# Four subtractions per unit move from VectorE to GpSimd in a two-layer encoder trunk

## The chip, the core and the metric

The kernel runs on one core of a Trainium2 chip. The metric is the device time of one execution in microseconds (us); before the change the median of three runs is 2601.45 us (2601.13 to 2602.01). PE is TensorE (matmul), PEld its weight load, DVE VectorE, ACT ScalarE, POOL GpSimd, and SP the queue that issues most of the DMAs.

## What is computed

Two layers over 1024 frames of width 1024 in float32: chunked attention in the first, a gated DeltaNet mixer in the second, and behind each a dense MLP with a residual. The change touches only the MLP, which runs twice:

```python
def squared_relu_mlp(h, w_up, w_down):      # h: 1024x1024, w_up: 1024x4096, w_down: 4096x1024
    return jnp.square(jax.nn.relu(h @ w_up)) @ w_down
```

## The kernel before

Every float32 operand of a product is split into a high part (ACT copies it to the matmul type, `high`) and a low part (the difference, `low`, on DVE or POOL), and a block product is three matmuls per 128 rows: high by high, high by low, low by high. The MLP's two products are blocked two by two with seven products instead of eight (a Strassen-Winograd scheme), so that sums of blocks are needed of weights and of activations.

**Up half** (`up`). It walks through 16 units; a unit takes two panels of `w_up`, 128 columns each. It makes seven block products of 12 matmuls (84 matmuls) in the order Y(11), Z(s1), Y(s2), X(12), Y(s3), Z(s4), Y(22). X's evacuation is the instruction `ssum<-acc` (L1172), and its start is taken as the unit's mark below ("X end"). `put` makes a quarter of the squared activations: add, then ReLU and scale on DVE (L1172, L1174), square on ACT (L1175). The four quarters of a unit are g00, g01, g11, g10. They go to DRAM (`gr`), and `combine` (L1073) makes four differences of them in tiles `c`: t1 = g01 - g00, t3 = g11 - g01, t2 = g11 - t1, t4 = g10 - t2. It splits each into high (ACT) and low (DVE, L1086) and writes both to DRAM (`gt`). `combine` is called at a unit's end for units 0 to 13, and its steps run beside the products of the next unit.

Beside a unit, `up_weights` (L1030) makes the next unit's weights: two loads of 512 KB into the two `wraw` buffers (SP), four sums on POOL (S1, S2, S3, a21: tiles `s` and the first half of the second `wraw`), and the splits: `whi`/`wlo` of 128x1024 for the first panel (w0) and the second (w1), `ahi`/`alo` of 128x512 for s1, s2, s3. There are two `wraw` buffers only, so a panel's load is issued when the `wlo` that reads the old panel last is done. Each engine works its instructions off in the order in which the program issues them; that order is set by where the generators (`sums`, `more`, `rest`) are advanced between the products.

**Down half** (`down`). 32 units of seven products of six matmuls; after each product a *step* advances the generators. `late` is one: after the last residual rows are loaded it runs `late_sums` (L1395), which loads the four quarters of units 14 and 15 back into the halves of `R` and `ssum`, makes the four differences in place, splits them and writes them to `gt`. Seven steps are one unit.

Of the kernel before, what the change touches and what calls it, by code (L numbers as in the profile page):

```python
# [11 lines left out]
ALU = mybir.AluOpType  # L12
# [8 lines left out]
HB = 512  # L21
# [186 lines left out]
class Trunk:  # L208
# [821 lines left out]
    def up_weights(self, i, n, ap, A):  # L1030

        raw = []
        for j in range(2):
            t = self.wp.tile([P, KT, P], F32, name=self.nm("wraw"), tag="wraw")
            self.wq.dma_start(t, self.a["w_up"][i, 2 * n + j])
            raw.append(t)
        a11, a12, a21, a22 = raw[0][:, :4], raw[0][:, 4:], raw[1][:, :4], raw[1][:, 4:]
        yield
        S1, S2, S3 = (ap.tile([P, 4, P], F32, name=self.nm("s"), tag=f"a{m}") for m in range(3))
        A["s1"], A["s2"], A["s3"] = (  # L1040
            [ap.tile([P, 4, P], F32R, name=self.nm("a" + z), tag=f"a{3 + 2 * m + y}")
             for y, z in enumerate(("hi", "lo"))] for m in range(3))
        w0, w1 = ([self.wp.tile([P, KT, P], F32R, name=self.nm("w" + z), tag="w" + z) for z in ("hi", "lo")]
                  for _ in range(2))
        A["11"], A["12"] = ([z[:, 4 * m : 4 * m + 4] for z in w0] for m in range(2))
        A["s4"], A["22"] = ([z[:, 4 * m : 4 * m + 4] for z in w1] for m in range(2))

        self.padd(S1, a21, a22)
        self.psub(S2, S1, a11)
        self.psub(S3, a11, a21)  # L1050
        self.psub(a21, a12, S2)
        yield

        self.high(A["s1"][0], S1)
        self.high(w0[0], raw[0])
        yield

        self.low(A["s1"][1], S1, A["s1"][0])
        self.low(w0[1], raw[0], w0[0])
        self.high(A["s2"][0], S2)  # L1060
        yield

        self.low(A["s2"][1], S2, A["s2"][0])
        self.high(A["s3"][0], S3)
        yield

        self.low(A["s3"][1], S3, A["s3"][0])
        self.high(w1[0], raw[1])
        yield

        self.low(w1[1], raw[1], w1[0])

    def combine(self, n, g, mp, gt, first):  # L1073


        nc = self.nc
        t = {z: mp.tile([P, S], F32, name=self.nm("c"), tag=f"x{4 * (n % 2) + k}") for k, z in enumerate(SUMS)}

        def sub(z, x, y):
            nc.vector.tensor_tensor(t[z][:, HB:], x, y, ALU.subtract)  # L1080

        def high(z):
            self.high(t[z][:, :HB].bitcast(F32R), t[z][:, HB:])

        def low(z):
            nc.vector.tensor_tensor(t[z][:, HB:].bitcast(F32R), t[z][:, HB:], t[z][:, :HB], ALU.subtract)  # L1086
            nc.sync.dma_start(gt[n, SUMS.index(z)], t[z])

        def keep(name, x):
            if n < 2:  # L1090
                h, l = ops[name][n] = self.part(ex, str(n + 2 * (name == "21")))
                self.high(h, x)
                self.low(l, x, h)

        ex, ops = first
        sub("t1", g[0, 1], g[0, 0])
        sub("t3", g[1, 1], g[0, 1])
        yield
        sub("t2", g[1, 1], t["t1"][:, HB:])
        sub("t4", g[1, 0], t["t2"][:, HB:])  # L1100
        high("t1")
        keep("11", g[0, 0])
        yield
        high("t3")
        low("t1")
        keep("21", g[1, 0])
        yield
        high("t2")
        low("t3")
        yield  # L1110
        high("t4")
        low("t2")
        yield
        low("t4")
        yield
# [279 lines left out]
    def late_sums(self, mp, gr, gt):  # L1395

        nc = self.nc
        last = 2 * KT
        u = self.new_R()
        s = self.np.tile([P, S], F32, name=self.nm("ssum"), tag="ssum")  # L1400
        hi = [mp.tile([P, HB], F32, name=self.nm("r"), tag=t) for t in ("r", "q1")]
        for n in (last - 2, last - 1):
            r = u[:, :HB], s[:, :HB], s[:, HB:], u[:, HB:]
            for k, x in enumerate(r):
                nc.sync.dma_start(x, gr[n, k])
            r11, r21, r22, r12 = r
            for _ in range(4):
                yield
            for k, (t, x, y) in enumerate(((r11, r12, r11), (r12, r22, r12), (r22, r22, r11), (r21, r21, r22))):
                nc.vector.tensor_tensor(t, x, y, ALU.subtract)  # L1410
                for _ in range(4):
                    yield
            for z, t in zip(("t1", "t3", "t2", "t4"), (r11, r12, r22, r21)):
                h = hi[0]
                hi.reverse()
                self.high(h.bitcast(F32R), t)
                for _ in range(2):
                    yield
                nc.vector.tensor_tensor(t.bitcast(F32R), t, h, ALU.subtract)
                yield  # L1420
                for k, x in enumerate((h, t)):
                    nc.sync.dma_start(gt[n, SUMS.index(z), :, k * HB : (k + 1) * HB], x)
                for _ in range(3):
                    yield
# [1233 lines left out]
```

## Time and profile before

| | |
|---|---|
| median of three runs | 2601.45 us |
| the profiled execution | 2599.54 us, of which the span of its instructions 2596.4 us |
| PE busy | 2478.9 us (95%) |
| DVE busy | 1962.4 us (76%) |
| ACT busy | 1209.4 us (47%) |
| POOL busy | 1099.2 us (42%) |
| up halves | about 600 to 877 us and 1971 to 2249 us of the span |
| down halves | about 880 to 1175 us and 2252 to 2560 us |

A row of the timeline gives start, duration, engine, line, operation, output and inputs; "x2" marks merged neighbours, and brackets give the idle time of the engine before it and what ended that. A duration is that of the whole instruction with whatever it waits for once it has begun, so the same instruction can show 0.68 us at one place and 1.78 at another. Matmuls are pipelined, and PE's idle time is small everywhere; it is read best from the distance between marks that return once per unit.

### The profile page before, as it was taken

The numbers are of one execution on the slowest core, as the hardware profiler recorded it, in microseconds if no ns is written. First come the engines' busy times: TensorE is split into PE (matmuls) and PEld (weight loads), VectorE is DVE, ScalarE is ACT, GpSimd is POOL, SyncE is SP. The second block draws the span as 40 slices with busy tenths as digits, with TensorE's granted clock in tenths as the row PEclk, the third lists the DMA queues.
The fourth block names the chain that finished last, engine by engine and source line by source line (L and its number), as shares of the span: only waits on it lengthen the run. The fifth ranks groups of instructions, "written<-read, shape, count | busy, mean of one in ns | idle before, by whom it ended". The sixth has DMA issues, their size and how long they took to land.

```text
span 2596.4 us, 36674 instructions
## 1 busy us (share of the span) xinstructions
PE 2478.9 (95%) x12638; PEld 2050.4 (79%) x12638; DVE 1962.4 (76%) x3425; ACT 1209.4 (47%) x2269; POOL 1099.2 (42%) x962
## 2 busy tenths in 40 slices
PE   8999999999999999998888999999899999999997
PEld 6888888787778777886666788888687777777885
DVE  6665656778888788878579976675678888788878
ACT  6666667545545433334663334333335545433333
POOL 2444456412233365566464333332412322356556
PEclk9999999999999999999998999999999999999998
DMA  4222224315555977743443121223324555977752
GB/s 162 67 68 78 61 85 145 134 67 190 195 206 208 348 228 239 235 146 110 119 137 109 53 79 60 64 77 114 114 82 162 199 203 192 346 232 257 232 163 81
DMA packets 193081, 392.42 MB, mean 151 GB/s; under 512 B 54960, under 2 KB 61552, under 8 KB 192896
## 3 DMA queue, kind: packets, MB, share of 16 engines
q1 hardware_dynamic: 176048, 355.46, 41.4%
q10 hardware_dynamic: 16848, 34.63, 3.4%
q8 instruction: 99, 1.62, 0.3%
q14 instruction: 86, 0.70, 0.1%
HBM read 254.06 MB, written 127.57 MB: 147 GB/s over the span
## 4 chain that ended last, share of the span: by engine, by line
PE 55%; DVE 16%; issue 5%; DMA 2%; ACT 2%; POOL 1%; SPq 0%; ACTq 0%; DVEq 0%; POOLq 0%
PE y L1008 21%; PE z L1008 9%; PE acc L163 8%; PE acc L1008 6%; PE tp L163 3%; PE s L163 3%; DVE c L1086 3%; DVE wlo L1014 2%; PE acc L279 2%; PE acc L278 2%; PE acc L277 2%; DVE x L1508 1%; DVE ft L163 1%; DVE ssum L1172 1%; DVE alo L1014 1%
## 5 line engine op out<-in xcount | busy, mean ns | idle before, releaser
L163 PE MATMUL acc<-xs,whi 128*128 128x512 f32 x1808 | 631.1, 412 | 10.3 <-DVE xp L163 9.7
L1023 POOL TENSOR_TENSOR s<-wraw 128x256 f32<-128x256 f32 (+1 forms) x93 | 88.3, 950 | 772.7 <-DMA wraw<-in_w_up_dram 427.5
L163 PEld LDWEIGHTS acc<-xs,whi 128*128 128x128 f32 x1808 | 333.0, 191 | 59.4 <-DVE xp L163 6.5
L163 PE MATMUL acc<-xs,wlo 128*128 128x512 f32 x896 | 368.4, 411 | 2.8 <-POOL wlo L163 2.8
L1008 PE MATMUL y<-xs,whi 128*128 128x512 f32 x1008 | 312.6, 391 | 6.6 <-DVE x L1508 3.2
L163 POOL TENSOR_TENSOR wlo<-wraw,whi 128x512 fp32r<-128x512 f32 x126 | 167.9, 1332 | 244.8 <-ACT whi L163 195.5
L1008 PEld LDWEIGHTS y<-xs,whi 128*128 128x128 f32 x1008 | 188.8, 188 | 48.9 <-DVE x L1508 4.9
L1008 PE MATMUL y<-xs,wlo 128*128 128x512 f32 x504 | 199.7, 396 | 9.2 <-DVE wlo L1014 8.7
L1014 DVE TENSOR_TENSOR wlo<-wraw,whi 128x512 fp32r<-128x512 f32 (+1 forms) x182 | 198.8, 1092 | 8.5 <-ACT whi L1017 8.5
L1017 ACT ACTIVATE whi<-wraw 128x512 fp32r<-128x512 f32 (+2 forms) x191 | 146.5, 767 | 123.9 <-PE y L1008 87.1
L1008 PE MATMUL y<-xs,a 128*128 128x512 f32 x732 | 189.4, 394 | 13.8 <-DVE x L1508 12.6
L1017 ACT ACTIVATE a<-s 128x256 fp32r<-128x256 f32 x122 | 63.9, 524 | 290.4 <-PE y L1008 144.3
L1508 DVE TENSOR_TENSOR x<-y,x 128x512 f32<-128x512 f32 x240 | 165.1, 688 | 39.0 <-PE y L1008 32.4
L163 PEld LDWEIGHTS acc<-xs,wlo 128*128 128x128 f32 x896 | 171.7, 192 | 28.4 <-POOL wlo L163 4.1
L1008 PEld LDWEIGHTS y<-xs,a 128*128 128x128 f32 x732 | 135.1, 188 | 51.8 <-DVE x L1508 22.4
L1008 PE MATMUL acc<-xs,whi 128*128 128x512 f32 x528 | 162.9, 390 | 0.0
L1008 PE MATMUL y<-xs,ahi 128*128 128x512 f32 x512 | 161.9, 397 | 0.9 <-ACT nt L1197 0.9
L1008 PE MATMUL z<-xs,whi 128*128 128x512 f32 x480 | 148.0, 389 | 0.0
L163 POOL TENSOR_SCALAR pr<-pr,rs 128x640 f32<-128x640 f32 (+4 forms) x128 | 88.6, 696 | 129.3 <-DVE rs L163 98.2
L163 DVE CUSTOM_DVE_ANT_0 pr<-sp,bias 128x640 f32<-128x640 f32 (+4 forms) x128 | 83.8, 654 | 63.6 <-PE sp L163 62.6
L1086 DVE TENSOR_TENSOR c<-c 128x512 fp32r<-128x512 f32 x112 | 131.6, 1192 | 0.0
L163 POOL TENSOR_TENSOR cy<-cy,cz 128x512 f32<-128x512 f32 x48 | 69.3, 1443 | 145.3 <-DVE cz L163 135.2
(340 smaller groups left out, 6154.6 us busy)
## 6 DMA issues: line engine op xcount, KB each, us to landing
xs<-gt SPq DMA_DIRECT2D x256, 256.0 KB, 4.6
gt<-c SPq DMA_DIRECT2D x112, 512.0 KB, 4.6
wraw<-in_w_up_dram SPq DMA_DIRECT2D x64, 512.0 KB, 3.9
wraw<-in_w_down_dram SPq DMA_DIRECT2D x64, 512.0 KB, 4.4
r<-gr SPq DMA_DIRECT2D x88, 256.0 KB, 3.4
wraw<-in_w_in_dram SPq DMA_DIRECT2D x32, 512.0 KB, 3.5
gr<-ssum ACTq DMA_DIRECT2D x62, 256.0 KB, 2.0
wraw<-in_w_qkv_dram SPq DMA_DIRECT2D x30, 512.0 KB, 3.4
```

Source lines behind the costliest of these rows:

```text
L163: return call(*args, **more)
L277: nc.tensor.matmul(ps, hi[:, k], xh, start=(k == 0), stop=False)
L278: nc.tensor.matmul(ps, hi[:, k], xl, start=False, stop=False)
L279: nc.tensor.matmul(ps, lo[:, k], xh, start=False, stop=(k == KT - 1))
L1008: nc.tensor.matmul(ps, w[:, k], x, start=bool(first and f), stop=bool(last and e), skip_group_check=True)
L1014: self.nc.vector.tensor_tensor(lo, src, hi.bitcast(F32), ALU.subtract)
L1017: self.nc.scalar.activation(hi, src, AF.Copy)
L1023: self.nc.gpsimd.tensor_tensor(out, x, y, ALU.add)
L1086: nc.vector.tensor_tensor(t[z][:, HB:].bitcast(F32R), t[z][:, HB:], t[z][:, :HB], ALU.subtract)
L1172: nc.vector.tensor_tensor(g, c, t, ALU.add)
L1508: nc.vector.tensor_tensor(x, ps, x, ALU.add)
```

## The change

Three edits. (1) In `combine` the four differences are made on POOL (`psub`, L1020) instead of DVE; their splits stay. (2) In `late_sums` the four differences of units 14 and 15 are made on POOL as well; the first stands 14 steps behind the loads instead of 4, and they stand 3 steps apart instead of 4. (3) In `up_weights` for the third unit on, the last two sums S3 and a21 are issued one step after S1 and S2. All lines from 1050 on move by 1 to 4.

```diff
@@ up_weights
         self.padd(S1, a21, a22)
         self.psub(S2, S1, a11)
-        self.psub(S3, a11, a21)
-        self.psub(a21, a12, S2)
+        if n == 1:
+            self.psub(S3, a11, a21)
+            self.psub(a21, a12, S2)
         yield
...
         self.high(A["s2"][0], S2)
+        if n > 1:
+            self.psub(S3, a11, a21)
+            self.psub(a21, a12, S2)
         yield
@@ combine
         def sub(z, x, y):
-            nc.vector.tensor_tensor(t[z][:, HB:], x, y, ALU.subtract)
+            self.psub(t[z][:, HB:], x, y)
@@ late_sums
-            for _ in range(4):
+            for _ in range(14):
                 yield
             for k, (t, x, y) in enumerate(((r11, r12, r11), (r12, r22, r12), (r22, r22, r11), (r21, r21, r22))):
-                nc.vector.tensor_tensor(t, x, y, ALU.subtract)
-                for _ in range(4):
+                self.psub(t, x, y)
+                for _ in range(3):
                     yield
```

What that makes of the instruction order, first on DVE at the end of a middle unit of the first up half (unit 6, near 708 us; `g` and `ssum` are the quarters, `c` the differences, `wraw_7745` the second panel of the next weights). Before:

```order
L1172 TENSOR_TENSOR g_6885<-z_7710,nt_7764 128x512
L1174 SCALAR_TENSOR_TENSOR g_6885<-g_6885,R_6833 128x512
L1014 TENSOR_TENSOR alo_7787<-s_7782,ahi_7786 128x512
L1174 SCALAR_TENSOR_TENSOR g_6886<-y_7709,R_6833 128x512
L1080 TENSOR_TENSOR c_7860<-g_6885,ssum_6884 128x512
L1080 TENSOR_TENSOR c_7862<-ssum_6884,g_6885 128x512
L1014 TENSOR_TENSOR alo_7789<-s_7783,ahi_7788 128x512
L1080 TENSOR_TENSOR c_7861<-ssum_6884,c_7860 128x512
L1080 TENSOR_TENSOR c_7863<-g_6886,c_7861 128x512
L1014 TENSOR_TENSOR wlo_7793<-wraw_7745,whi_7792 128x1024
L1086 TENSOR_TENSOR c_7860<-c_7860 128x512
L1086 TENSOR_TENSOR c_7862<-c_7862 128x512
```

The same place on DVE now:

```order
L1176 TENSOR_TENSOR g_6885<-z_7710,nt_7764 128x512
L1178 SCALAR_TENSOR_TENSOR g_6885<-g_6885,R_6833 128x512
L1014 TENSOR_TENSOR alo_7787<-s_7782,ahi_7786 128x512
L1178 SCALAR_TENSOR_TENSOR g_6886<-y_7709,R_6833 128x512
L1014 TENSOR_TENSOR alo_7789<-s_7783,ahi_7788 128x512
L1014 TENSOR_TENSOR wlo_7793<-wraw_7745,whi_7792 128x1024
L1090 TENSOR_TENSOR c_7860<-c_7860 128x512
L1090 TENSOR_TENSOR c_7862<-c_7862 128x512
```

The four differences are gone from DVE, and `wlo` of the second panel stands directly behind the last `alo`.

On POOL, from the same unit's weight sums to the next unit's. Before:

```order
L1023 TENSOR_TENSOR s_7781<-wraw_7745 128x512
L1020 TENSOR_TENSOR s_7782<-s_7781,wraw_7743 128x512
L1020 TENSOR_TENSOR s_7783<-wraw_7743,wraw_7745 128x512
L1020 TENSOR_TENSOR wraw_7745<-wraw_7743,s_7782 128x512
L1023 TENSOR_TENSOR s_7939<-wraw_7903 128x512
L1020 TENSOR_TENSOR s_7940<-s_7939,wraw_7901 128x512
L1020 TENSOR_TENSOR s_7941<-wraw_7901,wraw_7903 128x512
L1020 TENSOR_TENSOR wraw_7903<-wraw_7901,s_7940 128x512
```

Now:

```order
L1023 TENSOR_TENSOR s_7781<-wraw_7745 128x512
L1020 TENSOR_TENSOR s_7782<-s_7781,wraw_7743 128x512
L1020 TENSOR_TENSOR s_7783<-wraw_7743,wraw_7745 128x512
L1020 TENSOR_TENSOR wraw_7745<-wraw_7743,s_7782 128x512
L1020 TENSOR_TENSOR c_7860<-g_6885,ssum_6884 128x512
L1020 TENSOR_TENSOR c_7862<-ssum_6884,g_6885 128x512
L1020 TENSOR_TENSOR c_7861<-ssum_6884,c_7860 128x512
L1020 TENSOR_TENSOR c_7863<-g_6886,c_7861 128x512
L1023 TENSOR_TENSOR s_7939<-wraw_7903 128x512
L1020 TENSOR_TENSOR s_7940<-s_7939,wraw_7901 128x512
L1020 TENSOR_TENSOR s_7941<-wraw_7901,wraw_7903 128x512
L1020 TENSOR_TENSOR wraw_7903<-wraw_7901,s_7940 128x512
```

The differences stand between two units' weight sums; the sums themselves keep their order, S3 and a21 directly behind S1 and S2, so edit (3) moves no instruction on POOL.

In the down half of the first block, DVE's rows around the first late difference (in `R`) before (`x` is the residual that a product is added to, `a` a low part of the next weights):

```order
L1508 TENSOR_TENSOR x_9130<-y_9659,x_9130 128x512
L1508 TENSOR_TENSOR x_9130<-acc_9658,x_9130 128x512
L1410 TENSOR_TENSOR R_9668<-R_9668 128x512
L1014 TENSOR_TENSOR a_9715<-s_9686,a_9714 128x256
L1508 TENSOR_TENSOR x_9132<-y_9659,x_9132 128x512
```

POOL's rows from the same difference on now, ten steps later (`xs` are lows of reloaded quarters, `s` and `wraw` weight sums):

```order
L1020 TENSOR_TENSOR R_9668<-R_9668 128x512
L1023 TENSOR_TENSOR s_9861<-wraw_9839 128x256
L1020 TENSOR_TENSOR s_9862<-s_9861,wraw_9839 128x256
L1012 TENSOR_TENSOR xs_9872<-r_9852,xs_9872 128x512
L1020 TENSOR_TENSOR s_9861<-wraw_9839 128x256
L1020 TENSOR_TENSOR wraw_9839<-wraw_9839,s_9862 128x256
L1020 TENSOR_TENSOR R_9668<-ssum_9669,R_9668 128x512
L1012 TENSOR_TENSOR xs_9896<-r_9854,xs_9896 128x512
L1020 TENSOR_TENSOR ssum_9669<-ssum_9669,R_9668 128x512
```

Before, a difference stood on DVE between two additions to the residual; now the four stand on POOL between the lows of reloaded quarters and the weight sums.

## Rows read from the trace of the kernel before

**Rows 1.** The page, busy time of each engine over the span.

```profile
PE 2478.9 (95%) x12638; PEld 2050.4 (79%) x12638; DVE 1962.4 (76%) x3425; ACT 1209.4 (47%) x2269; POOL 1099.2 (42%) x962
```

**Rows 2.** Timeline of PE inside a product: start, us, engine, line, operation.

```profile
702.05 0.61 PE L1008 MATMUL z<-xs,whi 128*128 128x512 f32 x2
...
702.73 0.61 PE L1008 MATMUL z<-xs,whi 128*128 128x512 f32 x2
```

**Rows 3.** Waits of PEld, 560 to 880 us: total us, times, longest.

```profile
PEld y L1008 <- DVE wlo L1014: 10.0, 14, 1.7
PEld y L1008 <- ACT nt L1197: 5.6, 15, 0.8
```

**Rows 4.** Timeline of DVE, the unit mark "X end" in both up halves.

```profile
639.77 0.69 DVE L1172 TENSOR_TENSOR ssum<-acc,nt 128x512 f32<-128x512 f32 x1 [2.97 <-PE acc L1008]
...
738.18 0.69 DVE L1172 TENSOR_TENSOR ssum<-acc,nt 128x512 f32<-128x512 f32 x1 [3.01 <-PE acc L1008]
...
758.05 0.69 DVE L1172 TENSOR_TENSOR ssum<-acc,nt 128x512 f32<-128x512 f32 x1 [2.99 <-PE acc L1008]
...
816.83 0.69 DVE L1172 TENSOR_TENSOR ssum<-acc,nt 128x512 f32<-128x512 f32 x1 [2.97 <-PE acc L1008]
...
836.09 0.69 DVE L1172 TENSOR_TENSOR ssum<-acc,nt 128x512 f32<-128x512 f32 x1 [2.97 <-PE acc L1008]
...
855.64 0.69 DVE L1172 TENSOR_TENSOR ssum<-acc,nt 128x512 f32<-128x512 f32 x1 [2.97 <-PE acc L1008]
...
2011.41 0.69 DVE L1172 TENSOR_TENSOR ssum<-acc,nt 128x512 f32<-128x512 f32 x1 [3.01 <-PE acc L1008]
...
2228.48 0.69 DVE L1172 TENSOR_TENSOR ssum<-acc,nt 128x512 f32<-128x512 f32 x1 [3.00 <-PE acc L1008]
```

**Rows 5.** Timeline of POOL, the first weight sum (S1) of three units.

```profile
718.42 1.29 POOL L1023 TENSOR_TENSOR s<-wraw 128x512 f32<-128x512 f32 x1 [13.33 <-DMA wraw<-in_w_up_dram]
...
738.31 1.29 POOL L1023 TENSOR_TENSOR s<-wraw 128x512 f32<-128x512 f32 x1 [13.48 <-DMA wraw<-in_w_up_dram]
...
816.11 1.29 POOL L1023 TENSOR_TENSOR s<-wraw 128x512 f32<-128x512 f32 x1 [12.60 <-DMA wraw<-in_w_up_dram]
```

**Rows 6.** Timeline of DVE and POOL at 604 us, where they overlap.

```profile
604.33 1.78 DVE L1014 TENSOR_TENSOR alo<-s,ahi 128x512 fp32r<-128x512 f32 x1
...
605.64 1.61 POOL L1020 TENSOR_TENSOR wraw<-wraw,s 128x512 f32<-128x512 f32 x1
...
606.03 2.30 DVE L1014 TENSOR_TENSOR wlo<-wraw,whi 128x1024 fp32r<-128x1024 f32 x1
```

**Rows 7.** Timeline of DVE at the end of unit 6.

```profile
709.22 0.68 DVE L1174 SCALAR_TENSOR_TENSOR g<-y,R 128x512 f32<-128x512 f32 x1
709.82 0.68 DVE L1080 TENSOR_TENSOR c<-g,ssum 128x512 f32<-128x512 f32 x1
...
711.02 0.68 DVE L1014 TENSOR_TENSOR alo<-s,ahi 128x512 fp32r<-128x512 f32 x1
...
713.01 1.22 DVE L1014 TENSOR_TENSOR wlo<-wraw,whi 128x1024 fp32r<-128x1024 f32 x1
```

**Rows 8.** Timeline of ACT and of SP's issues at the same place.

```profile
708.73 0.63 ACT L1175 ACTIVATE g<-g 128x512 f32<-128x512 f32 x1 [3.10 <-DVE g L1174]
...
711.03 1.06 ACT L1017 ACTIVATE whi<-wraw 128x1024 fp32r<-128x1024 f32 x1 [0.46 <-ACT g L1175]
...
707.45 7.14 SPq L1035 DMA_DIRECT2D wraw<-in_w_up_dram  x2
```

**Rows 9.** Windows with late differences: length, then busy PE, PEld, DVE, ACT, POOL.

```profile
930.00:1050.00 120.00, 116.56 (x502) 92.94 (x501) 103.12 (x148) 39.94 (x74) 70.06 (x67) 1.00 0.71 229
...
2300.00:2430.00 130.00, 126.57 (x546) 101.21 (x545) 111.23 (x159) 43.27 (x80) 77.91 (x74) 1.00 0.72 231
```

**Rows 10.** Timeline of DVE and PE around the first late difference.

```profile
932.07 0.87 DVE L1410 TENSOR_TENSOR R<-R 128x512 f32<-128x512 f32 x1
...
935.04 0.73 PE L1008 MATMUL y<-xs,whi 128*128 128x512 f32 x2 [0.89 <-DVE x L1508]
```

## Prediction

> **What bounds the kernel now.** The page first: PE is busy 95% of the span, DVE 76%, POOL 42% [rows 1]. So DVE's sum of work is not the limit; what counts is where PE waits. In an up half I took two distances. Inside a product three matmuls follow each other in 0.68 us (702.05 to 702.73) [rows 2], so the 84 matmuls of a unit need 84 x 0.68 / 3 = 19.04 us. The marks "X end" stand 215.87 us apart over 11 units in the first block (639.77 to 855.64) and 217.07 in the second (2011.41 to 2228.48) [rows 4]: 19.62 and 19.73 us per unit. PE loses 0.58 and 0.69 us per unit, and the waits say to whom: to the low part of the first weight panel on DVE, and to ACT's copies of y and z, which come behind the same DVE work [rows 3].
>
> Why is that low part late? DVE stands idle about 3 us ahead of X end [rows 4], then has a chain to do between X end and `wlo`, and just then POOL makes the weight sums. The rows at 604 us show how the two engines get in each other's way: `alo` takes 1.78 us, POOL's next sum ends 1.14 us after `alo` has ended (606.11 to 607.25), and `wlo` ends 1.08 us after that (608.33) [rows 6]. Alone `alo` takes 0.68, `wlo` 1.22 [rows 7] and a POOL sum 1.29 [rows 5]. So two instructions that read two SBUF tiles on DVE and POOL take turns, each waiting for the other's to end. Hence it matters when POOL's run begins. Two units of the trace show the size: with S1 0.13 us behind X end (738.31 against 738.18) the next mark came after 19.87 us (758.05), with S1 0.72 us ahead of it (816.11 against 816.83) after 19.26 (836.09) [rows 4, 5]. The earlier the weight sums, the more of them falls into DVE's idle 3 us.
>
> **What sets S1.** Its second panel. The load can be issued when the `wlo` of the old second panel is done: that row ends at 713.01 + 1.22 = 714.23 [rows 7], the second of the two issues ends at 707.45 + 7.14 = 714.59 [rows 8], S1 begins at 718.42 [rows 5], 4.19 us behind `wlo`'s end. And `wlo` stands on DVE behind the four differences, while its high part was there at 711.03 + 1.06 = 712.09 [rows 8].
>
> **Part 1: the differences of units 0 to 13 on POOL.** It takes 14 x 4 = 56 subtractions per block, 112 in all, from DVE. That DVE time itself (112 x 0.68 us) is worth nothing, since DVE waits 3 us per unit anyway [rows 4]. Worth something is when `wlo` ends, so I walk through unit 6. g01's square ends at 708.73 + 0.63 = 709.36 [rows 8]; t1 can start at 709.4 and, at 1.3 us, ends at 710.7. `alo` is ready when the row at 709.22 ends, 709.90 [rows 7], waits for t1 and takes about 0.6 more: 711.3. t3 has waited and takes 1.14 [rows 6]: 712.45. `wlo` is ready at 712.09, waits to 712.45 and takes 1.08 [rows 6]: 713.5, against 714.23 now. Then t2 to 714.7, the first `c` low to 715.3, t4 to 716.45, the second `c` low to about 717.0. So the panel is freed 0.7 us earlier, and S1, 4.19 behind it, begins at 717.7; POOL's queue is empty at 716.45, 1.2 us before. DVE is done 1.4 us before the next mark. ACT's highs of the four differences now wait for POOL, but each difference is there before ACT comes to it, with over half a microsecond to spare in this walk.
>
> How sure is the 0.7? `wlo` waits for none or for all of one POOL subtraction, so it ends between 712.09 + 1.08 = 713.2 and 712.09 + 1.14 + 1.08 = 714.3: S1 from 1.0 us earlier to 0.1 later. I take 0.7, from the walk.
>
> With S1 0.7 us ahead of X end the nearest measured unit has 19.26 us. At that pace 11 units take 211.86 us: 4.0 us less in the first block, 5.2 in the second, together 9.2. The bounds: nothing lost on PE at all, 11 x 19.04 = 209.44, is 6.4 + 7.6 = 14.0 us less; no shift is 0. Three more places per block I count as cancelling: units 2 and 14 at the ends of the run gain like the others (0.4 each), unit 1, where the differences of unit 0 stand before the same `wlo` on POOL in a crowded place, may lose up to one POOL subtraction of wait (1.14 us of S1, some 0.8 us of period by the two measured units).
>
> **Part 2: the late differences.** 16 subtractions leave DVE in the down halves, at up to 0.87 us each [rows 10], and 16 come to POOL at 1.3. In the two stretches with late differences PE is idle 120 - 116.56 = 3.44 and 130 - 126.57 = 3.43 us [rows 9], partly because of the splits, which stay. The first difference shows the harm that one can do: behind it the addition to the residual came late and PE stood 0.89 us [rows 10]. On POOL a difference can still hold up a low on DVE by its 1.14 us, so part of that stays. Bounds: all idle time gone, 6.9 us less; or every one of the 16 costs 0.89, 14.2 us instead of 6.9, 7.3 more. I take 2 us less, nearer to no change, as on either engine a difference delays DVE by about the same. The 10 steps of delay themselves cost nothing: the results are read only in the unit before the last quarter of the down half, and 14 steps of six matmuls (1.36 us by [rows 2]) put 19 us between the loads and the first difference.
>
> **Part 3: the weight sums in two runs.** In the order of POOL nothing moves: S3 and a21 stand directly behind S1 and S2 as before. Zero.
>
> **Sum.** 9.2 + 2 = 11.2 us less. The profiled execution of before took 2599.54 us (span 2596.4), so 2588.3 by it; the median of the runs is 1.9 us above that execution, and on its scale it is 2601.45 - 11.2 = 2590.
>
> **A rule against the change.** A subtraction of this size takes 1.29 us on POOL [rows 5] and 0.68 on DVE [rows 7], a ratio of 1.9. The Trainium skill, "GPSIMD Engine Reference", section "Key points", says that for elementwise work the DVE is about twice as fast; the ratio here agrees. By that rule the differences were better left where they are; what would follow from it is the first rival.
>
> **Rivals.** *POOL's run is late (slower).* Place: POOL's queue, where S1 now stands behind t4. If all four differences had to wait for a DVE instruction of `wlo`'s size, they would take 4 x (1.30 + 1.08) = 9.5 us from 709.4 on, to 718.9, and S1 would begin 0.5 us later than now. From 718.42 on it decides. By the two measured units (0.61 us of period per 0.85 us of S1) that is 0.36 us per unit, 22 x 0.36 = 8 us more: 2609. Against it: only one `wlo` stands in that stretch of DVE [rows 7], and the walk ends at 716.45. Chance 0.12.
>
> *No shift (within 0.2%).* `wlo` meets a POOL difference that has just begun and ends at 714.3; the wait for POOL takes the place of the differences in its own queue, and S1 stays. Then only part 2 is left: about 2600. For it: the walk's 712.45 rests on steps of a few tenths. Chance 0.20.
>
> *The down half takes it back (within 0.2%).* Part 2 at its bad end, 7.3 more against 9.2 less: about 2600. Chance 0.06.
>
> **How the numbers follow.** My forecast has 0.62, the rivals 0.12, 0.20 and 0.06. About 0.2%, 5.2 us, is what a measurement here can tell from no change. Faster 0.62, within it 0.26, slower 0.12. The range takes in the best end of both parts (14.0 + 6.9, 2581) and the two rivals near 2600 with the scatter of the runs (2603); left out are the slower rival and a few hundredths.
>
> **What would show it.** Distance of the marks: 19.2 to 19.3 us instead of 19.62 and 19.73. S1 about 0.7 us ahead of X end in nearly every unit. `wlo` of the second panel directly behind POOL's second difference, at about 1.4 us. PEld's waits on DVE `wlo` clearly below 10.0 us. In the down stretches PE idle 2 to 3 us each. The prediction is wrong if `wlo` ends no earlier against X end, if S1 is released by POOL's own queue instead of the load, or if S1 comes earlier and the marks stay where they are.

## The result: 0.9912 of the time before

The changed kernel takes 2579.86 us in the median (2571.49 to 2582.57) against 2601.29 (2600.86 to 2602.01) beside it, a ratio of 0.9912 with a 95% interval of 0.9889 to 0.9935. That is 21.4 us less, where 11.2 were forecast: 2590, with a low end of 2581, so the median lies 1 us below the range. The direction and the place were right; the terms for both halves were too small. The profiled execution took 2579.18 us, its span 2577.4 (before 2599.54 and 2596.4).

The page's line of busy times, against [rows 1], shows about 199 us more on POOL and 48 less on DVE:

```profile
PE 2472.7 (96%) x12638; PEld 2063.6 (80%) x12638; DVE 1914.8 (74%) x3297; ACT 1210.1 (47%) x2269; POOL 1298.2 (50%) x1090
```

The marks "X end" of the changed kernel, the same four as the ends in [rows 4] (timeline: start, duration, engine, line, operation, tiles; in brackets the idle time before):

```profile
641.82 0.69 DVE L1176 TENSOR_TENSOR ssum<-acc,nt 128x512 f32<-128x512 f32 x1 [1.30 <-PE acc L1008]
851.79 0.69 DVE L1176 TENSOR_TENSOR ssum<-acc,nt 128x512 f32<-128x512 f32 x1 [1.79 <-PE acc L1008]
2003.83 0.69 DVE L1176 TENSOR_TENSOR ssum<-acc,nt 128x512 f32<-128x512 f32 x1 [1.29 <-PE acc L1008]
2213.30 0.69 DVE L1176 TENSOR_TENSOR ssum<-acc,nt 128x512 f32<-128x512 f32 x1 [1.53 <-PE acc L1008]
```

The two in each block stand 209.97 and 209.47 us apart, 19.09 and 19.04 per unit. 19.04 is what 84 matmuls need [rows 2]: over most of both up halves PE loses nothing any more. What the parts of the span took in the profiled executions, counted from mark to mark and to the last product of a down half (first block + second block):

| stretch | before | after | difference |
|---|---|---|---|
| up halves, marks of units 1 to 15 | 277.88 + 278.98 | 271.09 + 270.93 | -14.8 |
| down halves, mark 15 to last product | 331.95 + 328.11 | 328.90 + 325.00 | -6.2 |
| the rest of the span, of which the edits move only unit 0's four differences | 1379.5 | 1381.5 | +2.0 |

**The unit that the prediction walked through** (unit 6, the answer to [rows 5, 7, 8]): POOL's differences, DVE from the last `alo` to the next first panel's low, ACT's copy, and SP's two loads and two writes.

```profile
709.29 1.30 POOL L1020 TENSOR_TENSOR c<-g,ssum 128x512 f32<-128x512 f32 x1 [4.96 <-ACT g L1179]
710.55 1.74 POOL L1020 TENSOR_TENSOR c<-ssum,g 128x512 f32<-128x512 f32 x1
712.26 2.27 POOL L1020 TENSOR_TENSOR c<-ssum,c 128x512 f32<-128x512 f32 x1
714.61 1.80 POOL L1020 TENSOR_TENSOR c<-g,c 128x512 f32<-128x512 f32 x1
716.84 1.29 POOL L1023 TENSOR_TENSOR s<-wraw 128x512 f32<-128x512 f32 x1 [0.43 <-DMA wraw<-in_w_up_dram]
...
709.77 1.37 DVE L1014 TENSOR_TENSOR alo<-s,ahi 128x512 fp32r<-128x512 f32 x1
711.97 1.41 DVE L1014 TENSOR_TENSOR wlo<-wraw,whi 128x1024 fp32r<-128x1024 f32 x1 [0.83 <-ACT whi L1017]
714.57 2.39 DVE L1090 TENSOR_TENSOR c<-c 128x512 fp32r<-128x512 f32 x2 [1.19 <-POOL c L1020]
718.24 0.69 DVE L1176 TENSOR_TENSOR ssum<-acc,nt 128x512 f32<-128x512 f32 x1 [1.29 <-PE acc L1008]
724.59 1.21 DVE L1014 TENSOR_TENSOR wlo<-wraw,whi 128x1024 fp32r<-128x1024 f32 x1
...
710.87 1.06 ACT L1017 ACTIVATE whi<-wraw 128x1024 fp32r<-128x1024 f32 x1 [0.46 <-POOL c L1020]
...
707.29 6.44 SPq L1035 DMA_DIRECT2D wraw<-in_w_up_dram  x2
715.28 2.03 SPq L1091 DMA_DIRECT2D gt<-c  x2
```

The second panel's low ends at 713.38 (forecast 713.5), t4 at 716.41 (forecast 716.45): the walk holds to 0.2 us. But S1 begins at 716.84, not 717.7. The load takes 3.46 us from that low to S1, not 4.19. And the first write of a difference is issued at 715.28, 1.55 us behind the load's issue (713.73); before, it was issued at 714.85, 0.26 us behind it. With S1 1.40 us ahead of X end, the next first panel's low ends at 725.80, 7.56 us behind X end; before it was 8.67.

What waits in the first up half (waiter <- what it waited for: us, times, longest), against [rows 3]:

```profile
DVE wlo L1014 <- ACT whi L1017: 11.3, 13, 1.4
...
PEld y L1008 <- DVE wlo L1014: 4.6, 5, 1.8
...
PEld y L1008 <- ACT nt L1201: 2.5, 6, 0.6
```

PE's wait for `wlo` is less than half of 10.0. It is now DVE that waits, for ACT's copy of the second panel.

### The profile page after: what moved, and what is told of

It reads as the page before. It is cut to its first block, busy times and chain, and to the rows that moved or that the text cites. A ratio compares the mean times of both kernels' runs of the same rounds, so it can differ in the third digit from the quotient of the medians.

```text
span 2577.4 us, 36731 instructions
## 1 busy us (share of the span) xinstructions
PE 2472.7 (96%) x12638; PEld 2063.6 (80%) x12638; DVE 1914.8 (74%) x3297; ACT 1210.1 (47%) x2269; POOL 1298.2 (50%) x1090
## 4 chain that ended last, share of the span: by engine, by line
PE 61%; DVE 11%; DMA 3%; issue 3%; ACT 1%; POOL 1%; SPq 0%; ACTq 0%; DVEq 0%; POOLq 0%
PE y L1008 24%; PE z L1008 11%; PE acc L163 9%; PE acc L1008 6%; PE tp L163 4%; PE s L163 3%; DVE ft L163 2%; PE acc L279 1%; PE acc L277 1%; PE acc L278 1%; DVE x L1512 1%; DMA wraw<-in_w_up_dram 1%; DVE wlo L1014 1%; DVE fz L163 1%; DVE xs L393 1%
## 5 line engine op out<-in xcount | busy, mean ns | idle before, releaser
L1014 DVE TENSOR_TENSOR wlo<-wraw,whi 128x512 fp32r<-128x512 f32 (+1 forms) x182 | 209.4, 1151 | 27.3 <-ACT whi L1017 27.3
```

The costliest lines, as they stand in the source:

```text
L1014: self.nc.vector.tensor_tensor(lo, src, hi.bitcast(F32), ALU.subtract)
```

## Which time decides: a rule read from 308 units

PE does its products in a fixed order, so the date by which it needs the first panel can be worked out: X is the fourth product of seven, three more take 3 x 2.72 = 8.16 us, then the next unit's Y(11) reads the first panel (w0). I took, of 11 middle units in each of the two up halves, the end of w0's low against X end and the distance to the next mark, in all 14 profiles of this study. In 168 units with w0's low at 8.2 us or later, the next mark comes 11.02 to 11.13 us behind that low. In 140 units with it at 8.05 or earlier, the next mark comes after 19.03 to 19.07 us whatever S1 did. So the period is w0's low + 11.03, and at least 19.04; the bend is at 8.0 (no unit lies between 8.05 and 8.24). The 11.03 fits the order as well: from the low on Y(11), Z, Y and X follow, 4 x 2.72 = 10.88 us. Medians over the 22 units, in us against X end; "load lands after" is the time from the low's end to S1, and S1 begins 0.13 us behind the landing in every one of these units of the kernels without fillers:

| kernel | second panel's low ends | load lands after | S1 begins | w0's low ends | period (mean) |
|---|---|---|---|---|---|
| before | -4.19 | 4.17 | -0.02 | 8.67 | 19.68 |
| after | -5.20 | 3.38 | -1.77 | 7.64 | 19.07 |
| e1, POOL in the up half | -5.33 | 3.32 | -1.83 | 7.54 | 19.04 |
| e5, DVE, behind the panel | -5.49 | 3.33 | -2.03 | 7.51 | 19.05 |
| e6a, S1 held 3 fillers | -4.88 | 4.63* | -0.25 | 8.44 | 19.48 |
| e6b, S1 held 6 fillers | -4.87 | 6.37* | 1.50 | 9.63 | 20.66 |
| e7c, splits later | -4.24 | 3.32 | -0.92 | 9.96 | 21.05 |

(* S1 waits for POOL's fillers here, not for the load.) The two units that the prediction used, 19.87 and 19.26 [rows 4, 5], lie on this line as well (w0's low at 8.82 and 8.23). In the second of them the load took 3.46 us, against 3.94 to 4.34 in the other 21 units of the kernel before: its S1 was early by the load alone, so the landing time had moved already in the unit that the forecast took as its measure.

## The experiments

In the expectations A is the theory that the up half gains because the second panel's load, and with it S1, comes earlier; the other letters are its rivals, as they are described there.

**One edit at a time.** e1 is the edit in `combine` alone, e2 the one in `late_sums`, e3 the one in `up_weights`, each as in the diff above.

> Only the differences of units 0 to 13 go to POOL; the late ones stay on DVE as before. Theory A (the weight sums begin earlier, so PE loses less in the up halves): unit marks 19.0 to 19.1 us apart as in the changed kernel, down halves as before: 2601.3 - 14.8 (what the two up halves gained between the marks of units 1 and 15) = 2586.5 us. Rival B (the down halves gain because the up halves end differently, not through the late differences): the whole change, about 2580 us.

2586.11 us (2583.22 to 2587.01), ratio 0.9941 (0.9927 to 0.9956). The up halves take 541.0 us against 556.9 before and 542.0 with all edits; the second down half 328.9, against 328.1 before.

> Only the late differences go to POOL, 14 steps behind their loads. Theory A: unit marks 19.62 and 19.73 us apart as before, PE idle in the two stretches with late differences about 1.7 us instead of 3.4, so 3.4 us less: 2598 us, up to 5.7 less (2595.6) if all that the down halves gained comes from here. Rival B: 2601 us, no change.

2592.35 us (2587.48 to 2595.35), ratio 0.9968 (0.9957 to 0.9979): 8 us, more than I expected. The up halves are those of before (556.8); the down halves of its profiled execution, the slowest of its seven runs, took 657.2 us against 660.1, so that profile shows only 2.8 of the 8. More on this under Part 2 below.

> Only the weight sums are issued in two runs. Theory A: no instruction stands elsewhere, 2601.3 us within 0.1%. Rival: the two runs let DVE in between the sums, and the up halves gain several us, 2590 to 2597 us.

2601.08 us, ratio 0.9999 (0.9988 to 1.0009). The third edit alone does nothing. The 14.4 and 8.2 us of the first two add up to 22.6, which agrees with the 21.4 of the whole: e2's interval alone is 5.5 to 11.2 us.

**Is POOL needed in the up half?** e5 leaves the differences on DVE, and only puts them behind the second panel's low, from the third unit on:

```diff
+        yield
+        yield
         sub("t1", g[0, 1], g[0, 0])
         sub("t3", g[1, 1], g[0, 1])
-        yield
         sub("t2", g[1, 1], t["t1"][:, HB:])
         sub("t4", g[1, 0], t["t2"][:, HB:])
         high("t1")
-        yield
         high("t3")
+        yield
         low("t1")
...
```

> The kernel before, POOL untouched; from unit 2 on the four differences stay on DVE and only move behind the low part of the second weight panel, before the next mark, so DVE has the same work. Theory A (what counts is when the panel is freed and S1 begins): the low ends about 1 us earlier against the mark, S1 1.0 to 1.7 us earlier, unit marks 19.1 to 19.3 us apart, 8 to 13 us less: 2588 to 2593 us. Rival C (what counts is the DVE time that leaves): marks 19.6 to 19.7 us apart, 2601 us, or slower since the differences now stand just ahead of the mark.

2582.94 us (2580.36 to 2586.46), ratio 0.9932 (0.9917 to 0.9947); the up halves take 540.6. The same place in e5, DVE, then POOL, then SP:

```profile
710.22 1.22 DVE L1014 TENSOR_TENSOR wlo<-wraw,whi 128x1024 fp32r<-128x1024 f32 x1 [1.51 <-ACT whi L1017]
711.37 0.68 DVE L1080 TENSOR_TENSOR c<-g,ssum 128x512 f32<-128x512 f32 x1
...
717.05 0.69 DVE L1192 TENSOR_TENSOR ssum<-acc,nt 128x512 f32<-128x512 f32 x1 [1.86 <-PE acc L1008]
...
714.71 1.62 POOL L1023 TENSOR_TENSOR s<-wraw 128x512 f32<-128x512 f32 x1 [12.13 <-DVE c L1086]
...
705.54 6.26 SPq L1035 DMA_DIRECT2D wraw<-in_w_up_dram  x2
714.61 6.95 SPq L1087 DMA_DIRECT2D gt<-c  x3
```

No difference is on POOL, all four still cost DVE 0.68 us each, and the whole gain of the up half is there: the panel's low ends 5.6 us ahead of X end, S1 begins 2.3 us ahead of it. (The bracket at S1 names a low on DVE; the load landed at 714.58, 0.13 us ahead of S1, as in all middle units of e5.) What counts is what stands ahead of that low, not the engine. e5's first write also comes later, 2.80 us behind the load's issue in place of 0.26, so its S1 gains from both: 1.3 us by the low and 0.8 by the load.

**How much S1 may lose.** e6a and e6b are the changed kernel with 3 or 6 fillings of a tile (which S3 then overwrites) on POOL directly ahead of S1, from the fourth unit's weights on; they read nothing (e6b has 6 in place of 3):

```diff
+        if n > 2:
+            for _ in range(3):
+                nc = self.nc
+                nc.gpsimd.memset(S3, 0.0)
         self.padd(S1, a21, a22)
```

> The changed kernel with three fills of a 128x512 tile on POOL ahead of S1 (the tile is written over by S3 later), from the third unit's weights on: differences on POOL as changed, only S1 is held back. Theory A: S1 goes back toward the mark and the marks go apart with it, by the two units of the kernel before 0.7 us of period per us of S1, up to 19.7 us when S1 is at the mark: 2582 to 2594 us according to how long a fill takes. Rival C (the DVE time that left is what counts): marks stay at 19.05, 2580 us.

> As before with six fills. Theory A: S1 at or behind the mark, marks 19.7 us apart or more, 2594 us or more; the loss grows from three to six fills. Rival C: marks stay at 19.05, 2580 us.

e6a: 2587.75 us, ratio 0.996 (0.9944 to 0.9976). e6b: 2613.94, ratio 1.0063 (1.0046 to 1.0079). One unit of e6b:

```profile
723.25 3.45 POOL L1051 MEMSET s<- 128x512 f32 x6
726.66 1.66 POOL L1023 TENSOR_TENSOR s<-wraw 128x512 f32<-128x512 f32 x1
...
725.15 0.69 DVE L1180 TENSOR_TENSOR ssum<-acc,nt 128x512 f32<-128x512 f32 x1 [1.29 <-PE acc L1008]
733.58 1.21 DVE L1014 TENSOR_TENSOR wlo<-wraw,whi 128x1024 fp32r<-128x1024 f32 x1
745.86 0.69 DVE L1180 TENSOR_TENSOR ssum<-acc,nt 128x512 f32<-128x512 f32 x1 [1.33 <-PE acc L1008]
```

The second panel's low still ends 4.9 us ahead of X end there; only S1 is late, 1.51 us behind X end, and the unit takes 20.71 us. The gain goes as S1 goes, though the differences are off DVE in both of these kernels as well.

**Why does the load land sooner?** e7 wrote the calls that write t1 and t3 to DRAM later in the program; the queue's order came out as before (t1's write 0.27 us behind the load).

> The kernel before; from unit 2 on only the writes of t1 and t3 are issued a few us later (behind the high of t4), so that they no longer run beside the load of the second panel. Theory A2 (the faster landing, 3.46 us behind the low in the changed kernel against 4.19 before, comes from these writes being later): S1 0.5 to 0.8 us earlier, marks 19.3 us apart, 7 to 10 us less: 2591 to 2594 us. Rival: landing stays at 4.2 us, marks at 19.6 to 19.7, 2601 us.

2600.85 us, ratio 1.0005 (0.9994 to 1.0016), landing 4.18 us: a second reading of the kernel before, which tells nothing of its question. e7c asks it through the data: the low parts that the writes wait for stand later on DVE.

```diff
         high("t3")
-        low("t1")
         yield
         high("t2")
-        low("t3")
         yield
+        low("t1")
         high("t4")
-        low("t2")
+        low("t3")
         yield
+        low("t2")
         low("t4")
```

> The kernel before, in which from the third unit on the low parts of the four differences stand one or two steps later on DVE (t1 and t3 behind the next X end). The differences and the second panel's low stay, so the load of the second panel is issued as before, but the writes of t1 and t3, which in the kernel before are issued 0.27 us behind the load, come some 6 us behind it. Theory A2 (these writes slow the load down): the load lands 3.3 to 3.5 us behind the second panel's low instead of 4.0 to 4.3, S1 stands 0.7 us ahead of X end, the marks stand 19.1 to 19.4 us apart, and the run takes 2589 to 2596 us. Rival (the landing time has another cause): 4.0 to 4.3 us as before, S1 at X end, marks 19.6 us apart or, since one more low stands behind X end ahead of the first panel's, up to 20.2; 2600 to 2611 us.

The load lands after 3.25 to 3.43 us in 21 of 22 units, S1 stands 0.9 us ahead of X end: A2 holds for the landing. The DMA view of the 6 or 7 us around the load says it directly (tile, queue, issues, size of each, median time from issue to landing), first the kernel before with two writes of the same size behind the load, from 713 us on:

```profile
gt<-c SPq DMA_DIRECT2D x2, 512.0 KB, 5.0
wraw<-in_w_up_dram SPq DMA_DIRECT2D x1, 512.0 KB, 4.0
```

and e7c from 720 us on, with no write in the stretch:

```profile
wraw<-in_w_up_dram SPq DMA_DIRECT2D x1, 512.0 KB, 3.2
```

So two writes, the first issued 0.26 us *behind* a load, make the load land 0.8 us later (4.0 against 3.2 us). The Trainium skill, "DMA: Bandwidth & Descriptors", section "Issuing engines are not separate DMA queues", says that DMAs run on the same 16 DMA engines and interleave with each other; this pair of rows agrees and puts the price to it.

But the run took 2637.29 us (2630.57 to 2641.37), ratio 1.0141, far above what either theory expected. One unit of e7c, SP, POOL, DVE:

```profile
714.63 7.15 SPq L1035 DMA_DIRECT2D wraw<-in_w_up_dram  x2
729.67 5.78 SPq L1087 DMA_DIRECT2D gt<-c  x4
...
724.74 1.28 POOL L1023 TENSOR_TENSOR s<-wraw 128x512 f32<-128x512 f32 x1 [14.99 <-DMA wraw<-in_w_up_dram]
...
720.21 1.22 DVE L1014 TENSOR_TENSOR wlo<-wraw,whi 128x1024 fp32r<-128x1024 f32 x1
725.70 0.69 DVE L1192 TENSOR_TENSOR ssum<-acc,nt 128x512 f32<-128x512 f32 x1 [4.27 <-issue]
...
727.87 3.48 DVE L1086 TENSOR_TENSOR c<-c 128x512 fp32r<-128x512 f32 x2
...
734.40 1.22 DVE L1014 TENSOR_TENSOR wlo<-wraw,whi 128x1024 fp32r<-128x1024 f32 x1
```

Four lows of differences stand between X end and w0's low here, before there were two. The first two take 3.48 us between POOL's weight sums instead of 2 x 0.68, and w0's low ends 9.92 us behind X end: the next mark comes after 21.00. S1 came earlier and the kernel became slower. S1 is only the means; w0's low is what PE waits for.

**The down half.** e9 is the changed kernel with the late differences back on DVE at their new steps; e8 leaves them on POOL but 4 steps behind the loads instead of 14. First e9, then e8, both against the changed kernel:

```diff
-                self.psub(t, x, y)
+                nc.vector.tensor_tensor(t, x, y, ALU.subtract)
```

```diff
-            for _ in range(14):
+            for _ in range(4):
                 yield
```

> The changed kernel with the late differences back on DVE, but at their new steps (14 behind the loads, 3 apart). Theory A (the engine matters): PE idle in the two late stretches 3.4 us again instead of 1.7, 2583 to 2585 us. Rival D (their new place matters): 1.7 us as in the changed kernel, 2580 us.

> The changed kernel with the first late difference 4 steps behind its loads instead of 14, still on POOL and 3 steps apart. The two down halves took 660.1 us before and 653.9 after; with the late differences on DVE at the new steps 659.1. If the engine decides, the down halves stay at 653 to 655 us and the stretches with late differences keep about 1.7 us of PE idle time per 140; if the number of steps behind the loads decides together with the engine, POOL's differences at 4 steps wait for loads and hold up what stands behind them: 656 us or more.

e9: 2581.52 us (2579.62 to 2582.9), ratio 0.9934 (0.992 to 0.9949). e8: 2580.22 (2573.13 to 2581.6), ratio 0.9918 (0.9899 to 0.9938). Neither total is clear of the changed kernel's, and e9's alone would have said that the engine does not matter. The stretch with the late differences says otherwise (windows: length, PE busy, PEld, DVE, ACT, POOL busy, granted clock, DMA share, GB/s), first the kernel before, then the changed kernel, e9 and e8:

```profile
925.00:1065.00 140.00, 136.56 (x590) 109.48 (x589) 119.10 (x171) 45.98 (x85) 81.95 (x77) 1.00 0.72 234
```

```profile
925.00:1065.00 140.00, 138.27 (x606) 112.91 (x605) 115.53 (x167) 47.19 (x87) 93.78 (x87) 1.00 0.69 230
2285.00:2425.00 140.00, 138.27 (x606) 113.01 (x605) 115.88 (x167) 47.48 (x88) 95.19 (x89) 1.00 0.70 233
```

```profile
925.00:1065.00 140.00, 137.14 (x595) 110.57 (x594) 118.24 (x172) 46.74 (x87) 83.41 (x79) 1.00 0.70 230
```

```profile
925.00:1065.00 140.00, 138.11 (x601) 111.90 (x600) 116.15 (x166) 47.18 (x87) 93.83 (x87) 1.00 0.69 229
```

PE is idle 1.73 us with the differences on POOL, 1.89 with them on POOL at 4 steps, 2.86 on DVE at the new steps, 3.44 before, as in the shorter windows of [rows 9]. The second down half, which had the full granted clock in all of these, can be read from its mark 15 to its last product; before, then after, then e9:

```profile
2248.86 0.69 DVE L1172 TENSOR_TENSOR ssum<-acc,nt 128x512 f32<-128x512 f32 x1 [1.36 <-PE acc L1008]
2575.99 0.98 PE L1008 MATMUL acc<-xs,xs 128*128 128x256 f32 x6 [0.45 <-DVE x L1595]
```

```profile
2232.95 0.69 DVE L1176 TENSOR_TENSOR ssum<-acc,nt 128x512 f32<-128x512 f32 x1 [1.32 <-PE acc L1008]
2556.97 0.98 PE L1008 MATMUL acc<-xs,xs 128*128 128x256 f32 x6 [0.44 <-DVE x L1599]
```

```profile
2230.26 0.69 DVE L1176 TENSOR_TENSOR ssum<-acc,nt 128x512 f32<-128x512 f32 x1 [1.36 <-PE acc L1008]
2557.42 0.97 PE L1008 MATMUL acc<-xs,xs 128*128 128x256 f32 x6 [0.44 <-DVE x L1599]
```

328.11, 325.00 and 328.13 us; e8 has 325.79. So it is the engine that gives most of the 3 us: on DVE at the new steps the half gains nothing, though PE's idle time in the stretch falls by 0.6, and on POOL at the old depth it gains 2.3 of the 3.1. Other profiles with the granted clock at 1.00 in this half agree: late differences on DVE at the old steps took 328.1 to 329.2 us (before, e1, e3, e7), on POOL at the new ones 324.8 to 325.0 (after, e10, e11). Of the 3.1 us, 1.7 are PE's idle time in that stretch; where the other 1.4 sit I could not read, since PE's ends are modelled.

**Both gains without POOL in the up half, and the changed kernel once more.** e10 is e5's order with the second edit; e11 is the changed kernel.

> The differences of the up half stay on DVE but stand behind the second panel's low (from the third unit on), and the late differences are on POOL at the new steps: the two gains by other means than POOL in the up half. If S1's time and the late differences are all that counts, the marks stand 19.04 us apart, the up halves together take 540 to 541 us, the down halves 653 to 656, and the whole is the changed kernel's time less up to 1 us (2575 to 2583). If POOL's part in the up half is needed for something else, it is over 2585.

> The changed kernel once more, beside the one before it in this list: the two halves of both blocks as in its first profile within 1 us each (up 271.1 and 270.9, down 328.9 and 325.0). The stretch between them, which no edit touches, took 756.6 to 764.2 us in ten profiles; what the whole run differs from 2580 us should be found there.

e10: 2575.95 us (2571.2 to 2577.56), ratio 0.9905 (0.9887 to 0.9922). e11: 2578.51 (2578.22 to 2579.36), ratio 0.9918 (0.9901 to 0.9935). e10's up halves take 540.4 us against 542.7 in e11, since w0's low is at 7.92 or earlier in all its 22 units and in some of e11's at up to 8.39; its second down half is that of the changed kernel (324.8 against 325.0). It is the best of the study, but the two intervals overlap, so its lead over the changed kernel is not settled; over the kernel before it is.

e11's halves are those of the first profile within 1.6 us (I expected 1). The stretch between the last product of the first down half and the second block's mark 1, in which the kernels differ by no more than unit 0's differences, took 756.6 to 764.2 us in the 14 profiles, with a granted clock of 0.93 to 0.96 in the window from 1140 to 1480 us. This alone is 7.6 us, and most of the 11 us between the changed kernel's own runs may come from there; their traces were not taken, so that is argued, not shown.

## Why the prediction fell short, step by step

Up and down halves were forecast to gain 9.2 + 2 = 11.2 us and gained 21.0. Of the missing 9.8, 4.3 are the middle units of the up halves, 1.3 their edges, and 4.2 the late differences.

**What bounds the kernel, and the turn-taking.** Right: the marks went to the 19.04 us worked out from the matmuls, and the prediction's chain (second panel's low, load, S1, first panel's low) is the one that the experiments move. The turns of DVE and POOL are visible again: t2 takes 2.27 us on POOL beside `wlo`, 1.30 alone.

**The walk.** Right to 0.2 us for the panel's low and for all four differences in unit 6, and with it the cases against the first two rivals: POOL's queue is empty at 716.41, 0.43 us ahead of S1, and the panel's low ends at 713.38 and not at 714.3. The margin at POOL was thinner than the 1.2 us forecast, since the load landed sooner. The first rival's rate was about right: e6b's S1 stands 1.52 us later than before and a unit takes 0.98 us longer, 0.65 per us of S1, where 0.61 / 0.85 = 0.72 was used.

**"S1, 4.19 behind it, begins at 717.7": the step that failed first.** I took the load's landing as fixed. Of the step that moved I counted the subtractions and not the writes behind them: t1's and t3's splits wait for POOL now, so their writes are issued 1.55 us behind the load instead of 0.26, and the load lands 0.7 to 0.8 us sooner, the link that e7c shows. S1 moved by 1.75 us in the median, not 0.7: about 0.8 by the load, put at nothing, and 1.0 by the panel's low, put at 0.7.

**"At that pace 11 units": the term that was mis-sized.** 9.2 us were forecast for the 22 middle units, 5.90 + 7.60 = 13.5 were measured, just inside the bound of 14.0. The pace of 19.26 is right for an S1 0.7 us early (two units of the changed kernel with S1 0.68 and 0.62 early took 19.30 and 19.29). But a nearest unit gives one point of a line that bends; had I worked out by when PE needs w0's low (8.0 us behind X end) I should have seen that 19.26 is 0.2 us from the bend, and that any further gain on the load reaches 19.04.

**Edges.** The places counted "as cancelling" do not cancel: unit 14 gained 1.35 and 0.73, unit 2 lost 0.46 and 0.09, unit 1 lost nothing and 0.19. That is 1.3 us gained in all, where nothing was put down.

**Part 2.** 2 us forecast, 6.2 in the down halves. The sentence that failed is "on either engine a difference delays DVE by about the same": e9 and e8 separate the two, and what they show is that on POOL PE loses less. PE's idle time in the late stretch fell to 1.73 us, below the 2 to 3 that I had named. How much the first down half gained depends on the granted clock, and so it is open whether the bound of 6.9 held. It was 1.00 over that half before and 0.99 after, for a gain of 3.05. With the same late edit and 1.00 the half took 327.2 us in e10, 327.3 in e6a and 326.9 in e6b, 4.7 to 5.1 less than before, and with the 3.1 of the second block that is about 8 us, the size of e2's gain in the median (windows from mark 15 to the last product, before and e10):

```profile
876.45:1208.39 331.94, 318.47 (x1381) 257.26 (x1380) 274.58 (x387) 116.45 (x213) 192.09 (x183) 1.00 0.65 217
870.48:1197.64 327.16, 316.60 (x1381) 257.71 (x1380) 268.17 (x379) 116.44 (x212) 201.34 (x190) 1.00 0.65 219
```

With 0.99 on both sides (332.7 in e1 and 332.2 in e5 against 328.9, 330.4 and 329.9 in after, e11 and e2) it is 1.8 to 3.8 us. By which waits POOL spares PE is not shown row by row.

**Part 3.** Zero, as e3 shows.

**The range.** Its low end joined 14.0 and 6.9, a gain of 20.9; up and down halves gained 21.0 and the medians 21.4. So the low end was too high by about a microsecond. The 14.0 bounded the middle units only, and with the edges the up halves gained 14.8; the 6.9 was idle time of two windows, and the down halves together gained 5 to 8 us by these comparisons. I had also left the scatter of the runs out of the low end, though not out of the high one; the changed kernel's four runs lie between 2571.49 and 2582.57, on both sides of 2581.

## What to carry to other kernels

Work out by when the engine that sets the end needs each input, and put every chain against that date: behind it the period grew one for one here, ahead of it nothing changed. When a step moves, move its DMAs in the sum as well; a write issued just behind a load can be part of the load's time. And when totals scatter by as much as the effect, compare the stretch that the edit touches: e9's total hid 2 to 3 us per down half.

## What I had not expected of the hardware

A 512 KB load that was issued first lands after 4.0 us with two writes of that size behind it and 3.2 without. Single units do otherwise, and why is open: in the changed kernel the time from the low to S1 was once 4.59 us (before the mark at 698.94) with the first write 1.55 us behind the load as in its other units, in e7c once 4.10 with no write until after the landing, and in the kernel before once only 3.46 (before the mark at 816.83) with the write 0.27 us behind. Two differences on POOL beside `alo` and `wlo` on DVE took 1.74 and 2.27 us, so that the four took 7.1 us instead of 4 x 1.30, and this cost nothing, since the load for S1 landed later still.
